# RWKV and SGU trunk on one Trainium2 core: three more slots in the shared pool, an output projection unit split earlier, and four bank lists

## The chip, the cores and the metric

The kernel runs on one core of a Trainium2 chip. The time is device time in microseconds (us) from launch to the last instruction; the median of several runs counts. The kernel before takes 1320.23 us (three runs, 1316.43 to 1321.08).

The engines are named as in the profile: PE multiplies matrices into the eight banks of PSUM, DVE and ACT work element by element and move sums out of PSUM, POOL masks and fills, and SP issues nearly all DMAs. Every engine takes its instructions strictly in the order that was fixed when the program was built.

## The reference

Two layers on 512 tokens of width 1024, each a mixer and a SwiGLU feed-forward net, every sub-layer between two RMS norms. Layer 0 mixes with an RWKV-7 scan over 16 heads of 64, layer 1 with a gated product over blocks of 128 tokens. What matters here is the end of layer 0's mixer:

```python
def step(S, inp):
    r_t, w_t, k_t, v_t, a_t, b_t = inp
    sa = jnp.einsum('bhij,bhj->bhi', S, a_t)
    S = (S * w_t[:, :, None, :]
         + sa[..., None] * b_t[:, :, None, :]
         + v_t[..., None] * k_t[:, :, None, :])
    y = jnp.einsum('bhij,bhj->bhi', S, r_t)
    return S, y
...
y = _rwkv7_scan(r_h, decay, k_h, v_h, -kk, kk * a_h)
y = (y - mu) * lax.rsqrt(var + GN_EPS)                  # per head
y = y * gn_w + gn_b
y = y + jnp.sum(r_h * k_h * r_k, axis=-1, keepdims=True) * v_h
return (y * g) @ w_o
...
x = x + _rmsnorm(h, norm_gains[i, 1])
h = _rmsnorm(x, norm_gains[i, 2])
h = (jax.nn.silu(h @ w_gate) * (h @ w_up)) @ w_down
```

## The kernel before

All products keep nearly full float32 accuracy by three passes: each operand is split into a rounded part and the rest (`split`, L181 on ACT, L182 on DVE), and `mm3` (L206) adds three of the four products. So every weight tile is loaded (`wraw`), cast by ACT (`whi`) and subtracted by DVE (`wlo`) before PE can use it. `weight()` does this for one unit: a load of 512 KB, then the two halves of the split. `wraw`, and each pair of `whi` and `wlo`, have two buffers.

The scan is worked out in chunks of 64 tokens, for batches of 4 heads (b = 0 to 3; "B1" is the back of batch 1). The stages of a batch are:

- P and E: projections, decays and scaled operands, written to DRAM (`sa`, `sb`).
- F, `front`: loads four `MV` tiles (L988) and builds four `BX` tiles, one for each of 4 units, all 4 KB a partition from the shared pool `s` (`slot`, L175 to 178, with `SLOTS` tiles); then the key products `lm` (L1004) in the banks `pl`, from which ACT copies into `MV`, `LA` and `BX`, POOL masks, and PE transposes `bkt` (L1018).
- B, `back`: the inverse of each chunk's triangular matrix. DVE turns `LA` into `LX` (L1035), runs a loop of 30 small operations on `Dm` (L1049, L1051), and turns the result twice, into `hn` (L1054) and `Dt` (L1055). Then follows a chain of small products on PE with a copy by DVE or ACT behind each: Qp (L1071), `Qs` (L1074), Np (L1080) and Tp (L1083), their copies `Dn` (L1086) and `bdT` (L1088), Q2p (L1094), its copies (L1097, L1098), T2p (L1103), and the merge `bdT<-T2p` (L1107). Behind it, unit by unit, `mp` (L1112), its copy `MVt`, `gh` (L1119) and the adds into `MV` (L1121, L1122). `MVt` is first filled by the transposes `mvt` (L1062, bank list `pl`).
- S, the scan over 8 chunks: `us` (L1148), `su` (L1150, L1153), `Yp` (L1161).
- N, `finish`: group norm (L1177 to L1185), bonus, the transposes `vt` (L1198) and `yt` (L1223), gate (L206, L1227), and for b = 0 to 2 a store to `od`, which the projection loads again (`oraw`, L1281) and splits into `oT`.
- V, the value projection, gives PE work beside B0. Its `xs` (the shifted input) holds 4 slots of the pool until V3 is done.

`PLAN` (L35) gives the order in which these are written in the program. The sequence on each engine is not that order: the framework's scheduler fixes it at build time from its own estimates of durations, buffers and banks, so that a change of a pool's size or of a bank can move instructions over a wide stretch.

The output projection is `out_proj` (L287). It sums 8 k tiles for 4 token tiles into the banks of `h0` (columns 0 to 511) and later `h1` (columns 512 to 1023). `unit(half, u)` loads and splits the weights of two k tiles, and with `after` the scheduler is told to issue these no sooner than B3's merges (`merged0`, `merged1`, L1107). `acts(k)` gives `oT`. At its end each token tile is normed and transposed (`ptr`, L281, banks `tr`, copied out by L62 on ACT and L64 on DVE) for the feed-forward net, whose gate and up products `gu` begin in the banks of `gu`.

What is fixed by hand and touched by the change: `SLOTS`, `PLAN`, and the bank lists `BANKS_RWKV` and `BANKS_F0` (L28 to L30), in which the `pl` banks are 1 and 2, `pt` (the small products of the inverse) 3 and 4, `pb` 5 and 6, and `us`, `yp`, `mp` the banks 0, 7 and 5.

## Time and profile before

| what | value |
|---|---|
| median of 3 runs | 1320.23 us (1316.43 to 1321.08) |
| profiled execution | 1315.28 us |
| its span, first to last instruction | 1313.6 us |
| mean granted clock of PE | 0.984 |
| PE / weight loads / DVE / ACT / POOL busy | 96% / 83% / 75% / 56% / 12% |
| DMA, mean over the span | 110 GB/s, 144.29 MB |

A row of the timeline gives the start and the length in us, the engine, the line of the kernel, the operation, output<-input by tile names, the shape and the count; in brackets stand the idle time before it and what ended that. A row of the waits gives the engine and line that waited, what it waited for, the sum in us, the number of waits and the longest. PE's clock is granted in steps: at half rate a matrix product takes about twice as long, and the mean over a stretch is given as a share of full speed.

The page's slices show where PE is not at full use; each digit is one fortieth of the span (32.8 us) in tenths:

```profile
PE   5999999989899899999999999999989999999998
PEclk9999999999979999999999999999989999999999
```

The RWKV stages end near 380 us (twelfth slice), the output projection runs to 455 us (fourteenth), and then come the first feed-forward net, the gating unit and the second net.

### The profile page before, as it was taken

How to read it: one execution, taken by the hardware profiler on the slowest of the kernel's cores; microseconds unless marked ns; L12 is line 12 of the kernel's file. 1: busy time of each engine (PE TensorE's matmuls, PEld its weight loads, DVE VectorE, ACT ScalarE, POOL GpSimd, SP SyncE). 2: the span in 40 equal slices, each digit the busy share in tenths (PEclk: the TensorE clock that was granted, in tenths of full speed). 3: DMA queues.
4: the chain of work that ended last, by engine and by line, in shares of the span. 5: the costliest groups of instructions: out<-in, count | busy, mean ns of one | idle time of the engine just before them, and what ended most of it. 6: DMA issues, size and time to landing. Idle time of an engine off the chain costs nothing.

```text
span 1313.6 us, 24404 instructions
## 1 busy us (share of the span) xinstructions
PE 1257.4 (96%) x9644; PEld 1091.1 (83%) x9644; DVE 988.1 (75%) x1613; ACT 739.4 (56%) x1303; POOL 151.6 (12%) x300
## 2 busy tenths in 40 slices
PE   5999999989899899999999999999989999999998
...
PEclk9999999999979999999999999999989999999999
...
GB/s 163 34 95 175 146 224 156 88 72 65 75 127 112 75 80 160 68 126 125 92 154 136 122 49 128 94 135 94 144 97 1 129 98 105 120 125 149 113 65 81
DMA packets 219379, 144.29 MB, mean 110 GB/s; under 512 B 67920, under 2 KB 193408, under 8 KB 219264
## 3 DMA queue, kind: packets, MB, share of 16 engines
...
q8 instruction: 76, 1.25, 0.4%
...
## 4 chain that ended last, share of the span: by engine, by line
PE 68%; DVE 7%; ACT 2%; issue 1%; DMA 1%; POOL 0%; DVEq 0%; ACTq 0%
PE acc L206 25%; PE Q L206 10%; PE gu L206 9%; PE R L206 7%; PE Z L206 7%; PE u L206 3%; DVE wlo L182 1%; PE gh L1119 1%; PE mp L1112 1%; PE Yp L1161 1%; PE lm L1004 1%; DVE wsum L405 1%; DVE x L336 1%; PE s L1366 1%; PE ptr L281 0%
## 5 line engine op out<-in xcount | busy, mean ns | idle before, releaser
L182 DVE TENSOR_TENSOR wlo<-wraw,whi 128x1024 fp32r<-128x1024 f32 x83 | 103.1, 1244 | 66.5 <-ACT whi L181 57.7
L206 PE MATMUL Q<-bc,whi 128*128 128x256 f32 x816 | 147.3, 281 | 2.2 <-ACT hn L449 2.2
L206 PE MATMUL acc<-whi,ablk 128*128 128x512 f32 x448 | 141.6, 395 | 2.7 <-DVE acc L623 2.7
L181 ACT CAST whi<-wraw 128x1024 fp32r<-128x1024 f32 x83 | 86.9, 1050 | 101.5 <-PE acc L206 29.2
L206 PEld LDWEIGHTS Q<-bc,whi 128*128 128x128 f32 x816 | 125.5, 189 | 2.8 <-ACT hn L449 2.6
L181 ACT CAST whi<-wsum 128x1024 fp32r<-128x1024 f32 x68 | 71.1, 1051 | 85.0 <-PE Q L206 24.3
L206 PE MATMUL gu<-hT,whi 128*128 128x256 f32 (+1 forms) x448 | 112.0, 342 | 3.3 <-ACT hT L62 1.7
L206 PE MATMUL Q<-bc,wlo 128*128 128x256 f32 x408 | 114.6, 281 | 0.0
L206 PEld LDWEIGHTS acc<-whi,ablk 128*128 128x128 f32 x448 | 84.2, 188 | 23.3 <-ACT hn L621 1.8
L206 PE MATMUL Z<-bc,whi 128*128 128x256 f32 x544 | 99.8, 281 | 0.0
L206 PE MATMUL R<-bc,whi 128*128 128x256 f32 x544 | 98.7, 281 | 0.0
L182 DVE TENSOR_TENSOR wlo<-wsum,whi 128x1024 fp32r<-128x1024 f32 x68 | 82.2, 1221 | 21.5 <-ACT whi L181 20.4
L181 ACT CAST whi<-wq 128x1024 fp32r<-128x1024 f32 x51 | 53.5, 1050 | 72.3 <-PE R L206 22.9
L206 PEld LDWEIGHTS gu<-hT,whi 128*128 128x128 f32 x448 | 78.8, 197 | 13.7 <-ACT hT L62 2.4
L206 PE MATMUL acc<-wlo,ablk 128*128 128x512 f32 x224 | 88.5, 395 | 1.5 <-DVE wlo L182 1.5
L182 DVE TENSOR_TENSOR wlo<-wq,whi 128x1024 fp32r<-128x1024 f32 x51 | 65.3, 1284 | 27.6 <-ACT whi L181 27.4
L206 PEld LDWEIGHTS Z<-bc,whi 128*128 128x128 f32 x544 | 84.1, 189 | 0.0
L206 PEld LDWEIGHTS R<-bc,whi 128*128 128x128 f32 x544 | 83.8, 188 | 0.2
L206 PE MATMUL proj<-xsp,whi 128*128 128x512 f32 x256 | 82.4, 401 | 1.3 <-ACT r L813 1.3
L206 PEld LDWEIGHTS Q<-bc,wlo 128*128 128x128 f32 x408 | 77.2, 189 | 0.0
L206 PE MATMUL Z<-bc,wlo 128*128 128x256 f32 x272 | 76.3, 282 | 0.9 <-DVE wlo L182 0.9
L206 PE MATMUL R<-bc,wlo 128*128 128x256 f32 x272 | 76.6, 282 | 0.0
...
## 6 DMA issues: line engine op xcount, KB each, us to landing
...
```

The lines of the kernel that those rows point to most:

```text
L181: self.nc.scalar.copy(hi, src)
L182: self.nc.vector.tensor_tensor(lo, src, hi.bitcast(F32), op=ALU.subtract)
L206: self.nc.tensor.matmul(out, l, r, start=start, stop=stop, skip_group_check=resumed)
L336: v.scalar_tensor_tensor(xts[tt][:, c], f, y[:, 0:1], xts[tt][:, c], op0=ALU.mult, op1=ALU.add)
L405: v.tensor_tensor(s, x, y, op=ALU.add)
L1004: mm(lm[:, cc * P:(cc + 1) * P], st[:, cc].rearrange("p n t -> p (n t)"), mv[:, cc, :, hd, :], start=True, stop=True)
L1112: mm(mp[:, cc * P:(cc + 1) * P], bdT[:, q * NC + 4 * hh + cc].rearrange("p h t -> p (h t)"), mt[:, cc, :], start=True, stop=True)
L1119: mm(gh[:, cc * P:(cc + 1) * P], mt[rows, cc, :], bx[rows, 0:2, cc, :], start=True, stop=True)
L1161: mm(yp[yr, yc], MV[hh, q][:, cc, 1, hd, :], su[:, q, hd, :], start=True, stop=True)
L1366: mm(acc[:, tt * P:(tt + 1) * P], vt[tt][:, m * P:(m + 1) * P], wsT[:, m, :], start=True, stop=True)
```

## The change

- `SLOTS` goes from 17 to 20. Two fronts hold 8 tiles each (4 `MV`, 4 `BX`), and `xs` 4. The room, 12 KB a partition, comes from `dynamic_dma_scratch_size=4096`, the space for the descriptors of DMAs that POOL issues (9 in this kernel: the gains, and vectors and weights of the gating unit).
- `PLAN` gets "W1" behind "S0": the first unit of the output projection's weights (k tiles 0 and 1, columns 0 to 511) is loaded and split there, in the `wp` buffers that V has left, and is handed to `out_proj` as `ready`. The other units are issued behind B3's merges as before.
- `h0` becomes (1, 2, 5, 7): the first two token tiles' sums go into the banks of the key products (`pl`), which nobody needs behind F3 and its `mvt`. Before, the second tile's sum had bank 3, of B3's small products. `h1` and the banks of `gu` in the first feed-forward net are permuted to fit.

```diff
--- before.py
+++ after.py
@@ -26,13 +26,13 @@
 LN_EPS = 1e-5
 LN_HALF = -0.6931471805599453
 BANKS_RWKV = dict(pa=(0,), pl=(1, 2), pt=(3, 4), pb=(5, 6), pe=(0, 7, 3, 4), us=(0,), yp=(7,), mp=(5,), pf=(6,),
-                  h0=(1, 3, 5, 7), h1=(2, 4, 0, 6), tr=(1, 2))
-BANKS_F0 = dict(tr=(1, 2), gu=(3, 4, 7, 6), R=(3, 4), Q=(5, 0), Z=(7, 6), h0=(1, 2, 4, 0), h1=(3, 5, 7, 6))
+                  h0=(1, 2, 5, 7), h1=(4, 6, 0, 3), tr=(1, 2))
+BANKS_F0 = dict(tr=(1, 2), gu=(4, 6, 3, 7), R=(3, 4), Q=(5, 0), Z=(7, 6), h0=(1, 2, 4, 0), h1=(3, 5, 7, 6))
 BANKS_SGU = dict(tr=(1, 2), pa=(3, 5, 7, 6), h0=(1, 2, 4, 0), h1=(3, 5, 7, 6))
 BANKS_F1 = dict(tr=(1, 2), gu=(4, 0, 7, 6), R=(4, 0), Q=(3, 5), Z=(7, 6), h0=(1, 2, 0, 5), h1=(4, 3, 7, 6))
-SLOTS = 17
+SLOTS = 20
 E2 = 7
-PLAN = "P0 E0 P1 E1 P2 E2 P3 E3 X0 F0 B0 F1 V0 V1 V2 V3 B1 S0 F2 S1 F3 N0 B2 N1 B3 S2 N2 S3 N3".split()
+PLAN = "P0 E0 P1 E1 P2 E2 P3 E3 X0 F0 B0 F1 V0 V1 V2 V3 B1 S0 W1 F2 S1 F3 N0 B2 N1 B3 S2 N2 S3 N3".split()
 XV = "xxxessss"
 XSLOTS = 13
 LAG = 2
@@ -284,7 +284,7 @@
     def prenorm(self, col):
         return Norm(self, col)
 
-    def out_proj(self, acts, wrows, nk, row, xts, store=None, tail=3, norm=None, spare=None, mid=None, after=(), begun=None):
+    def out_proj(self, acts, wrows, nk, row, xts, store=None, tail=3, norm=None, spare=None, mid=None, after=(), begun=None, ready=()):
 
 
         nc = self.nc
@@ -303,6 +303,9 @@
 
         def unit(half, u):
             own = spare if half and u < nu - late[1] else None
+            if not half and u < len(ready):
+                hi, lo = ready[u]
+                return [(2 * u + j, (hi[:, j, :], lo[:, j, :])) for j in range(2)]
             with ExitStack() as order:
                 for ins in after:
                     order.enter_context(self.tc.issue_after(ins.ins))
@@ -1246,6 +1249,7 @@
             g_hidden()
             xk = mixed_split(1, "xxxxssss")
             xr, kr, ops, Y = None, {}, {}, {}
+            wo, begun_w = i["rwkv_w_o"][0].rearrange("(u j p) n -> u p j n", p=P, j=2), []
             for n in PLAN:
                 f, b = n[0], int(n[1])
                 if f == "P":
@@ -1262,6 +1266,8 @@
                     front(b, ops[b])
                 elif f == "B":
                     back(b, ops[b])
+                elif f == "W":
+                    begun_w.extend(self.weight(wo[u][:, :, 0:512]) for u in range(b))
                 elif f == "S":
                     if b == 3:
                         GW.append(gate_weights(b))
@@ -1289,9 +1295,8 @@
             xts = [self.xp.tile([P, D], F32, name="x", tag="x", bufs=TT) for _ in range(TT)]
             for t in range(TT):
                 nc.sync.dma_start(out=xts[t], in_=i["x"][0, t * P:(t + 1) * P, :])
-            wo = i["rwkv_w_o"][0].rearrange("(u j p) n -> u p j n", p=P, j=2)
             norm = self.prenorm("g02")
-            self.out_proj(acts, lambda u: wo[u], KT, i["norm_gains"][0, 1], xts, norm=norm, spare=e2, after=(ops[3]["merged0"], ops[3]["merged1"]))
+            self.out_proj(acts, lambda u: wo[u], KT, i["norm_gains"][0, 1], xts, norm=norm, spare=e2, after=(ops[3]["merged0"], ops[3]["merged1"]), ready=begun_w)
             return xts, norm
 
 
@@ -1417,7 +1422,7 @@
     import concourse.bacc as bacc
     from concourse.bass_utils import run_bass_kernel_spmd
 
-    nc = bacc.Bacc("TRN2", target_bir_lowering=False, num_devices=1)
+    nc = bacc.Bacc("TRN2", target_bir_lowering=False, num_devices=1, dynamic_dma_scratch_size=4096)
     arrays, ins = {}, {}
     for name in _INS:
         arr = np.ascontiguousarray(inputs[name])
```

The number of instructions on each engine is the same. PE's order is the same up to about 207 us, and behind about 470 us only neighbours change places. Between these, the following has moved.

DVE in B1's chain, from `Qs` on. Before:

```order
L1074 TENSOR_TENSOR Qs<-Qp,id_144 128x512
L1150 TENSOR_TENSOR su<-us,pc 64x2x64
L1088 COPY bdT<-Tp 32x16x32 x2
L1098 COPY Q_2991<-Q2p 32x512
L1177 TENSOR_REDUCE mu<-Y 128x16
L1178 TENSOR_SCALAR mu<-mu 128x16
L1179 TENSOR_TENSOR Y<-Y,mu 128x1024
L1183 TENSOR_REDUCE va<-hn 128x16
L1107 COPY bdT<-T2p 32x16x32
```

After (lines are 3 higher):

```order
L1077 TENSOR_TENSOR Qs<-Qp,id_144 128x512
L1153 TENSOR_TENSOR su<-us,pc 64x2x64
L1091 COPY bdT<-Tp 32x16x32 x2
L1153 TENSOR_TENSOR su<-us,pc 64x2x64
L1101 COPY Q_2991<-Q2p 32x512
L1153 TENSOR_TENSOR su<-us,pc 64x2x64
L1110 COPY bdT<-T2p 32x16x32
L1153 TENSOR_TENSOR su<-us,pc 64x2x64
L1124 TENSOR_TENSOR MV<-gh,BX 128x4x64
L1125 TENSOR_TENSOR MV<-gh,MV 128x4x64
L1180 TENSOR_REDUCE mu<-Y 128x16
```

The group norm's rows (`mu`, `Y`, `va`) stood between the copy `Q` and the merge `bdT<-T2p`; now the merge stands ahead of them. At the other end of B1, LX stood behind three pairs of the adds `MV` of B0, and stands right behind B0's merge now. Behind B1, LX of B2 now comes after the group norm of batch 0 has begun and after the adds of B1; LX of B3, all of its loop and two `oT` splits stand among the copies of B2's chain, ahead of its merge.

PE in B2's chain, from Q2p on to the first `mp`. Before:

```order
L1018 MATMUL bkt<-ident,ST 128x128 x4
L1094 MATMUL Q2p<-Dn_4024,LA 32x32
L1062 MATMUL mvt<-ident,MV 128x128 x4
L1094 MATMUL Q2p<-Dn_4024,LA 32x32 x18
L1062 MATMUL mvt<-ident,MV 128x128 x8
L1103 MATMUL T2p<-bdT,Q_4064 32x32 x19
L1062 MATMUL mvt<-ident,MV 128x128 x4
L1103 MATMUL T2p<-bdT,Q_4064 32x32 x13
L1198 MATMUL vt<-ident,hn 128x128 x4
L1062 MATMUL mvt<-ident,MV 128x128 x8
L1198 MATMUL vt<-ident,hn 128x128 x4
L1112 MATMUL mp<-MVt,bdT 128x128 x4
```

After:

```order
L1086 MATMUL Tp<-Dt,Qs 32x32 x64
L1097 MATMUL Q2p<-Dn_4030,LA 32x32 x32
L1201 MATMUL vt<-ident,hn 128x128 x4
L1106 MATMUL T2p<-bdT,Q_4070 32x32 x32
L1201 MATMUL vt<-ident,hn 128x128 x4
L1115 MATMUL mp<-MVt,bdT 128x128 x4
L1226 MATMUL yt<-ident,Y 128x128 x4
```

The transposes `bkt` and `mvt` that lay between the small products are now ahead of Tp (most of them inside Qp), with all of F3's key products. Before these rows, Np and Tp were mixed with key products and scan steps; now Tp is one piece.

PE in B3's chain, from the scan steps behind Qp on. Before:

```order
L1148 MATMUL us<-su,MV 64x64 x4
L1161 MATMUL Yp<-su,MV 64x64 x4
L1080 MATMUL Np<-Qs,Dt 32x32 x32
L1083 MATMUL Tp<-Dt,Qs 32x32 x64
L1094 MATMUL Q2p<-Dn_4507,LA 32x32 x32
L1148 MATMUL us<-su,MV 64x64 x4
L1161 MATMUL Yp<-su,MV 64x64 x5
```

After, with the program's numbers of the tiles, since the sums would read alike without them (`acc_5109` and `acc_5110` are the first two token tiles, `whi_3234` and `wlo_3235` the unit that was split early; two rows ahead and two behind are left out, the last sums go on with `oT_5130`):

```order
L1164 MATMUL Yp_4720<-su_4709,MV_3240 64x64 x2
L1164 MATMUL Yp_4720<-su_4709,MV_3245 64x64 x2
L206 MATMUL acc_5109<-whi_3234,oT_5115 128x512
L206 MATMUL acc_5109<-wlo_3235,oT_5115 128x512
L206 MATMUL acc_5109<-whi_3234,oT_5115 128x512
L206 MATMUL acc_5110<-whi_3234,oT_5115 128x512
L206 MATMUL acc_5110<-wlo_3235,oT_5115 128x512
L206 MATMUL acc_5110<-whi_3234,oT_5115 128x512
L206 MATMUL acc_5109<-whi_3234,oT_5130 128x512
L206 MATMUL acc_5109<-wlo_3235,oT_5130 128x512
L206 MATMUL acc_5109<-whi_3234,oT_5130 128x512
L206 MATMUL acc_5110<-whi_3234,oT_5130 128x512
```

Twelve sums stand between the scan steps behind Qp and Np; before, the first sum came behind T2p, one ahead of `mp` and eleven behind it.

At the end of the projection, before, PE's rows were: 27 sums, 3 transposes `ptr` of tile 0, 2 sums, 5 `ptr`, 7 sums, 8 `ptr` of tile 1, and then `gu`. After, they are: 8 `ptr` of tile 0, 36 sums, 8 `ptr` of tile 1, 26 products `gu`, 4 `ptr` of tile 2, `gu`.

## Prediction, made before the changed kernel was run

> **What bounds the kernel now.** I read the page first, then the waits of PE, then the granted clock by stretches, then PE's and DVE's timelines around the places found.
>
> ```profile
> PE 1257.4 (96%) x9644; PEld 1091.1 (83%) x9644; DVE 988.1 (75%) x1613; ACT 739.4 (56%) x1303; POOL 151.6 (12%) x300
> PE ptr L281 <- DVE hn L736: 7.5, 1, 7.5
> PE ptr L281 <- ACT hn L737: 5.6, 1, 5.6
> ```
>
> PE is busy for 96% of the span of 1313.6 us. The change adds and removes no PE work, so it can gain only where PE stands still or runs at a lower clock. 1313.6 − 1257.4 = 56 us are idle, of which 7.5 + 5.6 = 13 are the two first waits of the program, which the change does not reach. The rest is small waits, and behind them stretches at half clock:
>
> ```profile
> 225.00:240.00 15.00, 13.31 (x380) 12.82 (x379) 2.75 (x4) 7.28 (x16) 3.52 (x9) 0.89 0.06 20
> 285.00:300.00 15.00, 14.44 (x116) 13.13 (x117) 13.90 (x34) 9.04 (x19) 11.55 (x26) 0.89 0.09 20
> 315.00:330.00 15.00, 14.25 (x366) 12.10 (x355) 7.67 (x14) 12.54 (x34) 10.68 (x28) 1.00 0.28 81
> 330.00:345.00 15.00, 12.15 (x139) 10.27 (x138) 14.47 (x43) 7.19 (x13) 1.17 (x2) 0.89 0.09 32
> 360.00:375.00 15.00, 13.00 (x375) 12.02 (x376) 6.56 (x13) 9.35 (x20) 0.41 (x2) 0.53 0.15 33
> 450.00:465.00 15.00, 11.19 (x63) 9.40 (x62) 13.33 (x39) 10.90 (x30) 0.00 (x0) 0.89 0.36 105
> ```
>
> The columns are the stretch, its length, busy us of PE, weight loads, DVE, ACT and POOL, then the granted clock, the DMA share and GB/s. The rows from 225, 285, 330 and 360 hold the chains of the triangular inverses of batches 0 to 3 (B0 to B3), the last one the end of the output projection. A clock of 0.89 over 15 us is 0.11 × 15 × 2 = 3.3 us at half rate, which costs half of that, 1.7; 0.53 in B3 is 14 us, which cost 7. These places, 225 to 465 us, are what the change can move; from 470 us on the new order differs from the old by swaps of neighbours alone.
>
> **The change part by part.** Three more slots let a front (loads, key products) start before an older one's buffers come free, and the scheduler reorders B1, B2 and B3 with it.
>
> *B1.* These are rows of DVE, then of PE:
>
> ```profile
> 243.47 0.42 DVE L1121 TENSOR_TENSOR MV<-gh,BX 128x256 f32<-128x256 f32 x1 [5.99 <-PE gh L1119]
> 249.75 0.42 DVE L1121 TENSOR_TENSOR MV<-gh,BX 128x256 f32<-128x256 f32 x1 [4.85 <-PE gh L1119]
> 250.42 1.98 DVE L1035 STREAM_TRANSPOSE LX<-LA 128x1024 f32<-128x1024 f32 x1
> 279.36 1.22 DVE L1177 TENSOR_REDUCE mu<-Y 128x16 f32<-128x1024 f32 x1
> 283.56 1.22 DVE L1183 TENSOR_REDUCE va<-hn 128x16 f32<-128x1024 f32 x1 [1.18 <-ACT hn L1181]
> 284.81 0.69 DVE L1107 COPY bdT<-T2p 32x512 f32<-32x512 f32 x1
> 268.69 1.28 PE L1071 MATMUL Qp<-hn,LA 32*32 32x32 f32 x128 [0.47 <-DVE hn L1054]
> 270.56 0.30 PE L1161 MATMUL Yp<-su,MV 128*64 128x64 f32 x2 [0.60 <-issue]
> 275.95 0.59 PE L1083 MATMUL Tp<-Dt,Qs 32*32 32x32 f32 x46 [0.78 <-issue]
> 280.10 1.20 PE L1103 MATMUL T2p<-bdT,Q 32*32 32x32 f32 x64
> 285.56 1.77 PE L1112 MATMUL mp<-MVt,bdT 128*128 128x128 f32 x8 [2.24 <-DVE bdT L1107]
> ```
>
> Before, LX of B1 stands on DVE behind three pairs of adds that wait for PE, and DVE idles 5.99 + 4.85 us there. Now LX comes right behind B0's merge, since F1's key products are done by then, and B1's inverse can start earlier by up to 10.8 us of idle time; PE lets about half of it be used, since 8 of F2's key products and the scan of batch 0 still stand ahead of Qp. At the other end the group norm of batch 0 sat on DVE ahead of the merge `bdT<-T2p`: T2p ended at 281.3, the copy began at 284.81, PE waited 2.24, and 3.3 us at half clock followed. In the new order the group norm is behind the merge. The waits removed sum to 2.24 + 0.78 + 0.60 + 0.47 and 1.7 for the clock, 5.8. I take **−6**, ends 0 (DVE late for another reason) and −8 (with some of the other idle time).
>
> *B2.* The group norm and the adds that left B1's chain now stand before and in B2's:
>
> ```profile
> 324.12 1.95 DVE L1035 STREAM_TRANSPOSE LX<-LA 128x1024 f32<-128x1024 f32 x1 [0.53 <-POOL LA L972]
> 327.09 0.66 PE L1018 MATMUL bkt<-ident,ST 128*128 128x128 f32 x4
> 332.00 0.76 PE L1103 MATMUL T2p<-bdT,Q 32*32 32x32 f32 x36 [0.84 <-DVE Q L1098]
> 337.38 0.69 DVE L1107 COPY bdT<-T2p 32x512 f32<-32x512 f32 x1
> 338.12 1.16 PE L1112 MATMUL mp<-MVt,bdT 128*128 128x128 f32 x8 [0.52 <-DVE bdT L1107]
> 347.20 2.12 DVE L1054 STREAM_TRANSPOSE hn<-Dm 128x1024 f32<-128x1024 f32 x1
> ```
>
> From B1's merge (284.81) to B2's (337.38) pass 52.6 us. The work that the new order has on DVE between the two merges is 51.5 us, with the durations that the same rows have before. So B2's merge can follow B1's in the same time only if DVE is idle for 1.1 us in all; today it idles 7.3 of 15 us from 315 to 330 alone, where it waits for PE's scan steps. LX of B3 (1.95), its loop of 30 small operations, and two `oT` splits, which wait for a store and a load of `od`, now stand among the chain's copies. And PE has less to put between: before, 4 bkt and 24 mvt passes stood between Tp and `mp`, 28/4 × 0.66 = 4.6 us; now they are done ahead of Tp, and 8 vt passes, 1.3 us, are left. I take **+4**, that is two thirds of B1's gain given back. The ends are −2 (DVE keeps the lead, and the waits of 0.84 and 0.52 go) and +10 (4.6 for the cover, two more stretches at half clock at 1.7, and 2.12 if `hn` of B3 lands in the chain).
>
> *B3.* This is where the early weight unit and the two banks act:
>
> ```profile
> 360.10 1.25 PE L1080 MATMUL Np<-Qs,Dt 32*32 32x32 f32 x61 [1.44 <-DVE Qs L1074]
> 361.79 1.14 ACT L181 CAST oT<-oraw 128x512 fp32r<-128x512 f32 x2 [2.80 <-DMA oraw<-od]
> 364.48 0.42 PE L1083 MATMUL Tp<-Dt,Qs 32*32 32x32 f32 x12 [1.47 <-issue]
> 365.08 1.92 PE L1094 MATMUL Q2p<-Dn,LA 32*32 32x32 f32 x64 [0.18 <-ACT Dn L1086]
> 369.94 1.91 PE L1103 MATMUL T2p<-bdT,Q 32*32 32x32 f32 x62
> 443.22 0.39 PE L206 MATMUL acc<-wlo,oT 128*128 128x512 f32 x1
> 443.45 0.39 PE L206 MATMUL acc<-whi,oT 128*128 128x512 f32 x1
> ```
>
> Twelve sums of the output projection now stand between Qp and Np. From start to start one takes 443.45 − 443.22 = 0.23 us, so they are 2.8 us of work. They fill the wait of 1.44 and push Np back by the other 1.4, to 361.5. That push is free: Q2p waits for `Dn`, which ACT copies only behind the `oT` casts, and these waited 2.80 us for a DMA until 361.79; the new order leaves that queue as it was. So Q2p stays near 365, with 2.8 us of later work already done. What else there is to gain is the clock: T2p takes 1.91 here against 1.20 in B1. Of the 7 us that half clock costs I let one stretch of 3.3 go, 1.7 at most, and count somewhat under that: **−4**. The ends are −1 (the twelve sums take the place of idle time that comes back later) and −8 (the clock stays full up to `mp`).
>
> [...]
>
> *The end of the projection.* Before, PE ran out of sums while the normed activations were transposed:
>
> ```profile
> 454.89 0.66 PE L281 MATMUL ptr<-ident,x 128*128 128x128 f32 x4 [0.55 <-DVE hT L64]
> 456.64 0.66 PE L281 MATMUL ptr<-ident,x 128*128 128x128 f32 x4 [1.09 <-DVE hT L64]
> 458.24 0.62 PE L206 MATMUL gu<-hT,whi 128*128 128x256 f32 x3 [0.95 <-ACT hT L62]
> 460.07 0.58 PE L206 MATMUL gu<-hT,whi 128*128 128x256 f32 x1 [1.21 <-DVE hT L64]
> ```
>
> Tile 0's eight transposes now stand 36 sums (36 × 0.23 = 8.3 us) ahead of tile 1's, and the gate and up products start in banks that the first tiles' sums have left. The first two waits are covered, 1.64; of the other two, 2.16, and of the 1.7 of half clock that they bring, I count somewhat over a third, 1.4: **−3**, ends 0 and −5.
>
> *At nothing:* the early load and split. The split's 1.2 us on DVE and its cast on ACT fall into or ahead of B0's stretch, where DVE is busy for 2.75 of 15 us; without that cover they would cost 1.2. One more weight load stands in SP's queue ahead of the front's loads; these waited for slots there and no longer do, so the queue has the time. The smaller descriptor space serves DMAs that POOL issues, of which no one is on the chain: 0 (ends 0 and +2). The gate and up banks belong to the item above.
>
> Sum: −6 + 4 − 4 − 3 = **−9 us**. The profiled execution took 1315.28, so one like it would take 1306; the runs shown have the median 1320.23 (1316.43 to 1321.08), so I take the same step from there: **1311 us**.
>
> **The rivals.** *B2 takes it all.* If DVE idles between the merges as it does now, B2 costs +8; with B3's clock as low as before (−1) the sum is −6 + 8 − 1 − 3 = −2: **1318**. For it speaks that 1.1 us is all the slack; against it, that the wait at B2's `mp` is only 0.52 today.
>
> *DVE keeps its lead.* B1's whole gain goes on to B3 (−8 − 2 − 6 − 3 = −19): **1301**. For it speaks that DVE's idle time of 5.99 and 4.85 us is real; against it, that the 51.5 us must then run without a gap.
>
> *Slower: the bare chain in B2.* Between Tp and `mp` PE has only 1.3 us of other work left. If DVE is late there by a block of 2 us (an `hn`, an LX) at each of three copies, as the group norm made it in B1, PE stands 6 us, the 4.6 us taken out as cover have been spent where nothing was idle, and four stretches run at half clock (4 × 1.7 = 6.8): +17 in B2, with −6, −1 and −1 elsewhere +9: **1329**. It decides from a price of B2 of 14 on. Against it: B3, as bare today, loses 7 to the clock and 3.1 to waits, 10.
>
> *It doesn't do what it says.* If the twelve sums wait for their banks or for `oT`, Np stands behind them, since PE takes its instructions in order, and the inverse is late: +2 in B3 and a sum of −3, **1317**. The splits of batch 0's `oT` stand in B2's chain, well before, so this is unlikely, and I count it with the first rival.
>
> **How the numbers follow.** The forecast has 0.50 (its own range 1305 to 1316), B2 takes it all or B3 fails 0.28, DVE keeps its lead 0.12, slower 0.10. 0.5% is 6.6 us, about what a measurement of this kernel can tell from no change. Faster by more, below 1313.6: 0.46 of the first case and all of the third, 0.58. Within: 0.04, the 0.28 and 0.02 of the last, 0.34. Slower: 0.08. The range of 8 in 10 leaves out the slower case and the better part of the third: **1301 to 1321**.
>
> **What would show it.** B1: `mp`'s first wait for `bdT` under 0.5 us, at 276 to 278, and no half clock behind it. B2: the merge less than 5 us earlier than 337.38, and waits of PE from Tp to `mp` of over 3 us. B3: twelve sums between Qp and Np without a wait, Q2p still released by ACT's `Dn`, the clock of its 15 us above 0.6. End: the waits at the transposes gone and `gu` entered with at most one wait. The forecast is wrong if B2's merge is more than 5 us earlier (then lower), or if PE loses in B2 more than B1 gained (then higher).

## The result, and the profile after

The changed kernel takes **1330.62 us** (median of four runs, 1328.99 to 1332.54) against 1318.33 us (four runs, 1314.71 to 1321.08) for the kernel before: ratio **1.0103, 95% interval 1.0083 to 1.0122**. It is slower by 1%, where 0.7% faster was forecast. The profiled execution took 1329.26 us with a span of 1327.6 us, 14.0 us more than before. Of the profiles below one, that of e7, was taken in a slow execution (1350.26 us; its other three runs took 1330.21 to 1335.04), so only its order and its waits are read.

The page's line of busy times and the granted clock by stretches of the changed kernel, in the columns that the prediction explains; the stretches are those around the same chains, which now come up to 11 us later:

```profile
PE 1262.7 (95%) x9644; PEld 1096.3 (83%) x9644; DVE 988.3 (74%) x1613; ACT 738.2 (56%) x1303; POOL 151.9 (11%) x300
...
225.00:240.00 15.00, 12.24 (x348) 11.72 (x336) 3.66 (x5) 7.80 (x18) 5.96 (x15) 0.77 0.21 57
255.00:270.00 15.00, 12.94 (x240) 11.44 (x241) 10.20 (x25) 5.87 (x17) 6.10 (x15) 0.89 0.28 85
270.00:285.00 15.00, 12.38 (x376) 11.16 (x374) 2.40 (x5) 9.43 (x25) 5.26 (x14) 0.77 0.22 49
330.00:345.00 15.00, 8.49 (x330) 7.19 (x328) 12.99 (x34) 7.17 (x15) 0.36 (x2) 0.74 0.35 100
345.00:360.00 15.00, 13.65 (x113) 11.42 (x109) 12.70 (x27) 4.45 (x9) 0.00 (x0) 0.80 0.05 19
375.00:390.00 15.00, 13.52 (x224) 11.93 (x225) 6.26 (x10) 7.56 (x16) 0.41 (x2) 0.66 0.20 55
465.00:480.00 15.00, 13.54 (x89) 12.86 (x88) 14.46 (x52) 11.54 (x39) 0.00 (x0) 0.77 0.36 106
1035.00:1050.00 15.00, 11.96 (x79) 11.89 (x79) 12.11 (x12) 5.06 (x6) 0.00 (x0) 0.77 0.40 110
```

B0 and B1 (the rows from 225 and 270) went from 0.89 to 0.77: 0.23 x 15 x 2 = 6.9 us at half clock each, two stretches where there was one, and one more stands ahead of B1 (255), where the clock was full before. B2 (330 to 360) has 0.26 and 0.20, 13.8 us, against 3.3 before. Only B3 (375) is better, 0.66 for 0.53. The last row is new: the second feed-forward net lost clock, where before nothing happened.

PE's waits from 220 to 390 us, the changed kernel (what waited, for what, sum, number, longest):

```profile
PE Tp L1086 <- issue: 6.7, 4, 2.8
PE vt L1201 <- DVE hn L1198: 4.4, 1, 4.4
PE Yp L1164 <- DVE su L1153: 2.1, 1, 2.1
PE Q2p L1097 <- issue: 1.9, 1, 1.9
PE mp L1115 <- DVE bdT L1110: 1.3, 1, 1.3
```

8.6 us of these stand at "issue", where PE waited for nothing that the profile shows; in the same chains of the kernel before it is 5.3. The rest of these rows is DVE.

Where the 14 us lie, by PE's lost time: the length of a stretch less what its products need at their dense pace (the median from start to start of the same product in the trace of before). It holds waits and half clock together.

| stretch (B0's Qp to its mp, and so on) | lost before | after | difference | the prediction's term |
|---|---|---|---|---|
| start to B0's Qp | 31.2 | 30.2 | -1.0 | 0 |
| B0, Qp to mp | 5.4 | 7.0 | +1.6 | 0 |
| to B1's Qp | 3.4 | 5.8 | +2.4 | -6, with the next row |
| B1, Qp to mp | 6.9 | 8.9 | +2.0 | |
| to B2's Qp | 3.4 | 4.3 | +0.9 | +4, with the two next rows |
| B2, Qp to mp | 10.9 | 14.6 | +3.7 | |
| to B3's Qp | 1.4 | 2.5 | +1.1 | |
| B3, Qp to mp | 9.6 | 6.4 | -3.2 | -4 |
| to 15 us behind the first gu | 15.4 | 17.0 | +1.6 | -3 |
| to the second net's gu | 12.5 | 12.3 | -0.2 | 0 |
| second net, first 90 us | 2.9 | 7.1 | +4.2 | 0 |
| to the end | 3.0 | 3.9 | +0.9 | 0 |

From B0's first Qp to B3's first `mp` the differences sum to +8.5. PE's waits of over 0.15 us grew there from 13.1 to 18.3 us, of which those at issue by 3.3. The other 3.3 us are work that ran slower than its dense pace: the time at half clock in that stretch grew from 23.4 to 37.2 us. The table compares one profile with one; how far profiles of one order differ is said where it matters.

Rows of the changed kernel's timelines that carry most of it, six of PE and three of DVE:

```profile
233.13 0.44 PE L1086 MATMUL Tp<-Dt,Qs 32*32 32x32 f32 x16 [2.76 <-issue]
264.12 0.33 PE L1164 MATMUL Yp<-su,MV 128*64 128x64 f32 x2 [2.05 <-DVE su L1153]
277.16 1.17 PE L1097 MATMUL Q2p<-Dn,LA 32*32 32x32 f32 x36 [1.90 <-issue]
287.89 0.60 PE L1115 MATMUL mp<-MVt,bdT 128*128 128x128 f32 x3
464.78 1.32 PE L281 MATMUL ptr<-ident,x 128*128 128x128 f32 x8 [2.52 <-DVE x L339]
1038.11 0.58 PE L206 MATMUL Z<-bc,whi 128*128 128x256 f32 x1 [3.04 <-DVE bc L182]
...
260.11 2.05 DVE L1057 STREAM_TRANSPOSE hn<-Dm 128x1024 f32<-128x1024 f32 x1
262.06 1.89 DVE L1058 STREAM_TRANSPOSE Dt<-Dm 128x1024 f32<-128x1024 f32 x1
263.79 0.28 DVE L1153 TENSOR_TENSOR su<-us,pc 64x128 f32<-64x128 f32 x1
```

`mp` of B1 at 287.89 has no wait any more: the merge's 2.24 us went, as predicted. But B1's chain did not get shorter. From its first Tp to `mp` pass 15.7 us, against 11.3 before. And at 264.12 stands the price of the earlier inverse: the scan's `su` is queued on DVE behind `hn` and `Dt` of B1, which came forward past it, so that PE waits 2.05 us.

At 464.78 PE waits once for the normed tile, 2.52, where the prediction saw the first two of four small waits covered; of the other two, at `gu`, 0.37 and 1.09 us are left. At 1038.11 it waits 3.04 us in the second net for the split of `bc`. Two rows of DVE there show why:

```profile
1034.56 1.23 DVE L408 TENSOR_TENSOR wsum<-wq 128x1024 f32<-128x1024 f32 x1 [2.77 <-DMA wq<-in_ffn_w_up_dram]
...
1036.84 1.22 DVE L182 TENSOR_TENSOR bc<-tsum,bc 128x1024 fp32r<-128x1024 f32 x1
```

DVE stands 2.77 us before a sum of weights whose load has not come, and the split of `bc`, which PE waits for, is behind it. In the kernel before, the split stood ahead of that sum. This is one of the "swaps of neighbours" behind 470 us.

### The profile page after: what moved, and what is told of

Its sections match the earlier page's. It is cut to its first block, busy times and chain, and to the rows that moved or that the text cites. A ratio compares the mean times of both kernels' runs of the same rounds, so it can differ in the third digit from the quotient of the medians.

```text
span 1327.6 us, 24401 instructions
## 1 busy us (share of the span) xinstructions
PE 1262.7 (95%) x9644; PEld 1096.3 (83%) x9644; DVE 988.3 (74%) x1613; ACT 738.2 (56%) x1303; POOL 151.9 (11%) x300
## 3 DMA queue, kind: packets, MB, share of 16 engines
q8 instruction: 76, 1.25, 0.4%
## 4 chain that ended last, share of the span: by engine, by line
PE 74%; DVE 13%; ACT 4%; issue 4%; DMA 4%; SPq 1%; POOL 0%; DVEq 0%; ACTq 0%
PE acc L206 23%; PE Q L206 10%; PE Z L206 7%; PE gu L206 7%; PE R L206 6%; PE proj L206 5%; PE u L206 3%; DVE wlo L182 3%; PE v L206 2%; PE lm L1007 2%; PE gh L1122 1%; PE Yp L1164 1%; DVE wsum L408 1%; ACT whi L181 1%; DVE xs L769 1%
## 5 line engine op out<-in xcount | busy, mean ns | idle before, releaser
L206 PE MATMUL Z<-bc,whi 128*128 128x256 f32 x544 | 102.5, 286 | 3.0 <-DVE bc L182 3.0
L182 DVE TENSOR_TENSOR wlo<-wsum,whi 128x1024 fp32r<-128x1024 f32 x68 | 82.3, 1222 | 19.4 <-ACT whi L181 18.3
L206 PEld LDWEIGHTS gu<-hT,whi 128*128 128x128 f32 x448 | 77.4, 193 | 13.1 <-DVE hT L64 2.9
```

Of the source, the lines that this page charges most:

```text
L182: self.nc.vector.tensor_tensor(lo, src, hi.bitcast(F32), op=ALU.subtract)
L206: self.nc.tensor.matmul(out, l, r, start=start, stop=stop, skip_group_check=resumed)
```

## The experiments

Eighteen kernels. Each was timed beside the kernel before on the same chip; the ratio is to that. A diff shows what is edited, against the changed kernel or, where said, the kernel before.

### Which part of the change loses the time

**e1**: 20 slots and the smaller descriptor space, on the kernel before; no early unit, old banks.

```diff
-SLOTS = 17
+SLOTS = 20
-    nc = bacc.Bacc("TRN2", target_bir_lowering=False, num_devices=1)
+    nc = bacc.Bacc("TRN2", target_bir_lowering=False, num_devices=1, dynamic_dma_scratch_size=4096)
```

> Before, with twenty slots and the smaller descriptor space, but without the early weight unit and with the old banks. The order of the instructions in the chains of B0, B1 and B2 is that of the changed kernel; B3's chain and the second feed-forward net have the order of before. Theory (the slots' new order is what costs): PE loses in the trace of the changed kernel 11.7 us more than before from Qp of B0 to Qp of B3, so this kernel should be slower than before by 10 to 12 us, ratio 1.0075 to 1.009. Rival (the slots cost nothing, and the early unit, the banks or the late net cost): within 2 us of before, ratio 0.9985 to 1.0015.

Measured: 1330.84 us, ratio 1.0096 [1.0067, 1.0125], the whole loss of the change. It has the changed kernel's losses around B1 and in B2: 5.8 to B1's Qp, 8.5 in B1, 15.4 in B2. B0, in the changed kernel's order, loses 5.3 and has one stretch at half clock, as before. B3 loses 9.3 (9.6 before), and the first 90 us of the second net lose no more than before.

**e2**: the changed kernel with 17 slots, so the early unit and the four bank lists alone.

```diff
-SLOTS = 20
+SLOTS = 17
```

> The changed kernel with 17 slots: early weight unit, new banks, smaller descriptor space. The chains of B0 to B2 and the second feed-forward net have the order of before; twelve sums stand between Qp and Np of B3. Theory: only B3's gain is left, 3.2 us by the changed kernel's trace, and up to 2 more or less at the end of the projection: 2 to 5 us faster than before, ratio 0.996 to 0.9985. Rival (early unit or banks cost, as one more load and split stand ahead of B0's chain): slower than before by 2 us or more, ratio over 1.0015.

Measured: 1319.06 us, ratio 1.0012 [0.9985, 1.0039], no difference. B0 to B2 are as before within 0.5. B3 loses 5.5 for 9.6, a gain of 4.1, just the -4 of the prediction. But from B3's `mp` to the gate products 15.5 are lost for 12.3, and in the 15 us behind, 4.9 for 3.0: the gain is given back. Waits of PE in e2 from 374.7 to 464.7 us, behind B3's `mp`:

```profile
PE ptr L281 <- DVE hT L64: 2.5, 1, 2.5
PE Yp L1164 <- ACT Y L1166: 2.0, 1, 2.0
PE gu L206 <- DVE hT L64: 1.9, 1, 1.9
```

The last scan steps wait 2.0 us for ACT, and from 414.7 to 424.7 the clock is 0.83, 3.4 us at half. PE has one wait of 2.5 and one of 1.9 at the end of the projection in place of four of 0.55 to 1.21.

**e10**: the early unit alone, with 17 slots and the old banks and descriptor space (the diff is against the kernel before; the code that hands the unit over and the edit of e3, below, are in it too).

```diff
-PLAN = "... V3 B1 S0 F2 ...".split()
+PLAN = "... V3 B1 S0 W1 F2 ...".split()
```

> 17 slots, the old banks and the old descriptor space; the early weight unit alone, with the order of e3 in the second FFN. Six sums of the projection (1.4 us) stand between Qp and Np of B3. Theory (the sums drawn forward lie in time that B3 loses; what e2 gave back at the projection's start came of the sums of two tiles missing there, which the new banks let go forward): B3 loses 7 to 8.5 against 9.6 before, the stretch from mp to gu 12 to 13.5 against 12.3; ratio 0.997 to 1.000. Rival (each sum drawn forward is missing behind mp, wherever its bank is): the stretch from mp to gu loses what B3 gains, 1.4 to 3 more, ratio 0.9995 to 1.002.

Measured: 1319.51 us, ratio 1.0012 [0.9995, 1.0029]. B3 lost 8.5 (9.6 before), and the stretch behind it 15.0 (12.3 before). That is the rival's number; but e11, which draws no sum forward, lost 15.0 there as well, so a single profile does not show that the missing sums are the cause.

**e4**: the smaller descriptor space alone, on the kernel before; its order is that of before.

```diff
-    nc = bacc.Bacc("TRN2", target_bir_lowering=False, num_devices=1)
+    nc = bacc.Bacc("TRN2", target_bir_lowering=False, num_devices=1, dynamic_dma_scratch_size=4096)
```

> Before, with nothing but the smaller descriptor space for the DMAs that POOL issues; every engine has the order of before. Theory (the descriptor space is of no account): the same time as before, ratio 0.9985 to 1.0015. Rival (POOL's DMAs or the fetches of instructions suffer from it): slower by 3 us or more, ratio over 1.002.

Measured: 1315.48 us, ratio 0.9991 [0.9962, 1.0021]. It costs nothing that shows; e1's loss is the slots'. Its profile also shows how far one order can spread: B0 lost 1.3 us more than in the kernel before, with 6.8 us at half clock for 3.4.

### The second feed-forward net

**e3**: the changed kernel, with the weight sum of that one place queued on DVE behind the split of `bc`.

```diff
...
-            o["s"] = wsum(o["a21"], o["a22"])
+            with ExitStack() as order:
+                if li == 1 and n == first + 1:
+                    order.enter_context(self.tc.issue_after(quads.done[5].ins))
+                o["s"] = wsum(o["a21"], o["a22"])
...
```

(`quads.done[5]` is that split; the lines that record it are left out.)

> The changed kernel with one constraint more for the scheduler: in the second feed-forward net the weight sum that waits for a load is issued behind the split of bc, as before. Elsewhere no instruction changes its place. Theory (in the changed kernel DVE waits there 2.8 us for the load, PE waits 3.0 for bc, and half clock follows): faster than the changed kernel by 4 to 6 us, so slower than before by 6 to 9, ratio 1.0045 to 1.007. Rival (the late load is chance, or the time comes back later): as the changed kernel, ratio 1.009 to 1.011.

Measured: 1330.09 us, ratio 1.0084 [1.0048, 1.0121]. The 6.0 us lost from 50 to 90 us of that net are 0.3, so the cause of the wait is shown (0.1 to 1.0 in the later kernels with this edit, but 3.7 in e5, where `Z` waits for another split); over its first 90 us 3.9 are lost for 7.1 (2.9 before). The total does not show it: the ten runs spread from 1319 to 1337, and in the profiled one the stretch from B0's `mp` to B1's Qp lost 9.7 for 5.8, with the same order. Seven kernels with one order up to there (e3, e6, e9, e12, e14, e15, e18) lost 5.1 to 9.7 in it. So a difference of 2 us in one stretch of one profile proves little, and the readings below need either a place or several runs.

All further kernels with 20 slots contain this edit.

### The waits at "issue"

In six traces (before, after, e1 to e4) the longer waits inside the chains fell on the same numbers of the matmul in PE's program, counted from the start, within 6, whatever stood there. After has them at 1485, 2242, 3111 and 3745. The trace's DMA part has two queues that bring instructions, q14 with 39 transfers, 0.32 MB, and this one:

```profile
q8 instruction: 76, 1.25, 0.4%
```

On q8, 76 transfers, 1.25 MB, so 16 KB each; PE has 9644 matmuls and as many weight loads, and 2 x 9644 / 76 = 254, so I take q8 for PE's. Each of these waits ends 1.2 to 1.6 us after a transfer of q8 has landed. A wait at issue need not be of this kind: that of `Yp` in B1 (0.56 to 0.60 us in before, e2 and e4) ends about 8 us after the last landing.

**e5**: shift the program by half a piece.

```diff
         nc.gpsimd.memset(self.ones, 1.0)
+        dummy = self.ps.tile([P, 512], F32, name="dummy", tag="b6", bufs=1)
+        for _ in range(32):
+            nc.tensor.matmul(dummy[0:32, 0:32], self.ident[0:32, 0:32], self.ident[0:32, 0:32], start=True, stop=True)
```

> The kernel of e3 with 32 small products (32x32, 64 passes with 64 weight loads) at PE's very start, while it waits for its first data; every engine's order is otherwise that of e3. The products' result is used by nothing. Theory (the stalls in the chains are PE waiting for its own instructions, which come in pieces of 256): each such stall moves back by exactly 64 passes in the program. In e3 they stand in B0 behind 102 passes of Tp, in B1 behind 28 of Q2p, in B2 behind 123 of Tp, in B3 behind 105 of Tp; here they should stand behind 38 of Tp, 92 of Tp, 59 of Tp and 41 of Tp (each within 3), with lengths of 1 to 3 us, and nothing at the old places but what a next piece brings. Rival (a stall belongs to the work at its place: the half clock, a bank, a weight): the stalls stay where they are in e3, within 3 passes. The time may go either way by up to 6 us, since only the places move: 1322 to 1336.

PE's timeline of e3, then of e5, the rows in the chains that waited for issue (the count behind x is what ran from the wait on; Tp has 128 passes, Q2p 64):

```profile
232.19 0.44 PE L1089 MATMUL Tp<-Dt,Qs 32*32 32x32 f32 x16 [1.80 <-issue]
280.50 1.17 PE L1100 MATMUL Q2p<-Dn,LA 32*32 32x32 f32 x36 [1.06 <-issue]
340.38 0.25 PE L1089 MATMUL Tp<-Dt,Qs 32*32 32x32 f32 x3 [2.35 <-issue]
378.91 0.53 PE L1089 MATMUL Tp<-Dt,Qs 32*32 32x32 f32 x21 [1.61 <-issue]
```

```profile
233.03 0.95 PE L1092 MATMUL Tp<-Dt,Qs 32*32 32x32 f32 x88 [0.53 <-issue]
236.60 0.57 PE L1103 MATMUL Q2p<-Dn,LA 32*32 32x32 f32 x25 [1.97 <-issue]
276.17 0.50 PE L1092 MATMUL Tp<-Dt,Qs 32*32 32x32 f32 x35 [2.30 <-issue]
334.27 0.77 PE L1092 MATMUL Tp<-Dt,Qs 32*32 32x32 f32 x67 [1.50 <-issue]
338.11 0.32 PE L1103 MATMUL Q2p<-Dn,LA 32*32 32x32 f32 x3 [2.08 <-issue]
378.88 0.53 PE L1103 MATMUL Q2p<-Dn,LA 32*32 32x32 f32 x22 [1.06 <-issue]
```

The waits stand behind 38 passes of Tp in B0, 91 in B1 and 59 in B2; predicted were 38, 92 and 59 (two passes of Tp that run among those of Np are left out of the counts). In B3 nothing is at 41 of Tp, and the next piece, 127 passes on, waits at 42 of Q2p. So the place is set by the number of the instruction, not by the work there. The time, 1329.53 us, ratio 1.0107 [1.0078, 1.0136], is no better: B1 lost 6.4 instead of 8.8, B3 9.5 instead of 7.2.

**e11**: the same 32 products in the kernel before.

> The kernel of before with the 32 small products of e5 at PE's start; every other order is that of before. Theory (pieces of 256 instructions): the stalls inside the chains move back by 64 passes: B0 from behind 13 passes of Q2p to behind 77 of Tp, B1 from 80 of Tp to 16 of Tp, B2's out of Q2p into Tp or its fillers, B3 from 114 of Tp to 50 of Tp, each within 3 and 0.7 to 2.5 us long. The time: between 1312 and 1322, since some boundaries come to lie in waits and others out of them. Rival: they stay where they are in before.

Measured: 1321.83 us, ratio 1.0028 [0.9996, 1.0060]. The waits moved to 75 of Tp in B0 (77 predicted) and 50 of Tp in B3 (50); in B1 only 0.25 us stands at 16 of Tp (16 predicted), and the next piece, 128 on, waits 1.68 us at 18 of Q2p. B2's wait in Q2p is gone, and a gap at two passes of T2p stayed where it was, so that one is of another kind. B1 lost 10.4 instead of 6.9; with 1.09 us at Qp it has three such waits, 3.0 us, where the kernel before has 1.0.

### B2

In all kernels below, merge to merge is DVE's second copy `bdT<-T2p` of B1 to that of B2, "other work" is PE's from the first Tp to `mp` that is not the chain's own 2.6 us, "DVE's other" the durations of what DVE does from Tp to its merge beside the chain's 2.8 us, summed (neighbouring rows overlap, so the sum is above the busy time).

| | merge to merge | Tp to mp | other work | DVE's other | lost, Qp to mp | ratio |
|---|---|---|---|---|---|---|
| before | 52.6 | 15.8 | 5.4 | 13.1 | 10.9 | 1 |
| after | 61.7 | 14.7 | 1.0 | 12.5 | 14.6 | 1.0103 |
| e3 (order as after) | 60.8 | 13.7 | 1.0 | 12.5 | 13.7 | 1.0084 |
| e6 filler out | 59.8 | 13.0 | 0 | 11.3 | 13.9 | 1.0099 |
| e9 cover in, with a bank's wait | 63.1 | 16.6 | 2.9 | 13.2 | 16.2 | 1.0129 |
| e12 cover in | 61.9 | 16.9 | 2.9 | 13.2 | 16.0 | 1.0091 |
| e14 cover in, filler out | 61.6 | 15.2 | 1.9 | 11.1 | 15.6 | 1.0123 |
| e15 DVE's loop out | 58.8 | 11.7 | 1.0 | 8.7 | 11.7 | 1.0090 |
| e18 loop out, cover in | 58.6 | 14.6 | 2.9 | 8.7 | 11.6 | 1.0124 |

**e6**: the largest single wait of B2, 4.38 us of `vt`, stands in PE's queue ahead of T2p and waits for DVE. The products with `hn` that feed it are queued behind B2's merge.

```diff
                 obs = []
+                order = ExitStack()
+                for n in (0, 1) if b == 1 else ():
+                    order.enter_context(self.tc.issue_after(ops[2]["merged%d" % n].ins))
                 for q in range(2):
                     v.tensor_tensor(Vn[:, :, q], ...)
...
+                order.close()
                 return obs
```

> The kernel of e3 with the bonus of batch 1 (its load, the two products on DVE and the eight vt passes on PE) issued only behind B2's two merges, so that none of it stands between Q2p and mp of B2. Theory (a filler that itself waits for DVE stands in PE's queue ahead of T2p and holds it): vt's wait (4.38 us in the changed kernel's profile, 2.7 in e3's) is gone, T2p waits for Q alone; lost in B2 from Qp to mp 9 to 11 us against 13.7 and 14.6; time 1322 to 1328, ratio 1.004 to 1.009. Rival (B2 lost its cover, and that is the cost): with 1.3 us less of other work between Tp and mp, B2 loses as much as before or more, 13.5 to 16, and the ratio stays at 1.009 or over.

Measured: 1329.84 us, ratio 1.0099 [1.0069, 1.0129]. PE's two longest waits of e6 from B2's first Tp to `mp`:

```profile
PE T2p L1109 <- ACT bdT L1094: 3.8, 1, 3.8
PE mp L1118 <- DVE bdT L1113: 2.2, 1, 2.2
```

and the last two copies of `bdT` ahead of T2p, of DVE and of ACT:

```profile
346.38 0.69 DVE L1094 COPY bdT<-Tp 32x512 f32<-32x512 f32 x1
347.10 0.58 ACT L1094 COPY bdT<-Tp 32x512 f32<-32x512 f32 x1 [2.04 <-DVE bdT L1094]
```

The filler's wait is gone, and T2p itself waits 3.8 us in the same place, for copies of `bdT` that DVE and ACT make in turn and of which DVE's came late. The rival was right: 13.9 lost. The wait with the largest number was not the cause; it stood where T2p would have waited.

**e7**: e6, and the group norm of batch 1 behind the merge too.

```diff
-                group_norm(Y, tts)
+                with ExitStack() as order:
+                    for n in (0, 1) if b == 1 else ():
+                        order.enter_context(self.tc.issue_after(ops[2]["merged%d" % n].ins))
+                    group_norm(Y, tts)
```

> As e6, with the group norm of batch 1 too issued behind B2's merges; DVE then has only the triangular loop of B3 (small operations under 0.5 us) and two oT splits among B2's copies. Theory (what is left of B2's loss is DVE's copies standing behind long operations): the merge's wait at mp goes (1.3 us), B2 loses 7 to 9; but the norm's 10 us now stand in or ahead of B3, whose Dt follows it, so that B3's Qp is reached up to 3 us later or B3 loses up to 3 more; time 0 to 4 us under e6. Rival (no cover): as for e6, B2 at 13.5 or more. Rival (DVE is the bound there, not the order): the sum of what is lost from B1's mp to B3's mp is the same as in e6 within 1 us, the loss only moves.

Measured: 1334.85 us, ratio 1.0126 [1.0093, 1.0160]. T2p still waits 3.0 us for `bdT` and `mp` 2.5 for the merge. In the place of the norm, B3's loop and `Dt` came forward on DVE.

**e9** and **e12**: put cover back. Half of B2's `mvt` passes are written behind Q2p and queued behind the last Tp (e9). In e12, B3's `mvt` passes are held behind B2's last T2p as well.

```diff
...
+                for hh in range(2 - late, 2):
+                    with self.tc.issue_after(last.ins):
+                        turn(hh)
                 T2p = self.bank("pt", "T2p")
...
```

(`turn(hh)` is the old `mvt` loop for one half, `late` is 1 for B2, `last` the last Tp.)

> The kernel of e3 with half of B2's mvt passes (those of the second half of the chunks) issued only behind its last Tp, so that 16 mvt passes (4 x 0.58 = 2.3 us of PE work, 8 of them B2's) stand between Q2p and T2p again. Theory (B2 lost its cover: from Tp to mp the chain of copies takes 13 to 15 us whatever PE does in it, and the slots took 4.4 of the 5.4 us of other work out): from Tp to mp 13.5 to 15 us as in e3, the other work in it 1.0 -> 3.3 us, lost from Qp to mp 10.5 to 12 against 13.7; time 1324 to 1329, ratio 1.006 to 1.010. Rival (PE's queue or DVE's lengthens with what is put in, as B1's did, 11.3 -> 15.7 us with 2.2 us more): from Tp to mp 16 us or more and 13.5 or more lost, ratio as e3's or over.

Measured, e9: 1335.63 us, ratio 1.0129 [1.0095, 1.0163]. Its third `mvt` unit waited 3.7 us for its bank, since the key products have only two; so e9 tells nothing of cover.

> e9 with B3's mvt passes held behind B2's last T2p: only the 8 mvt passes of B2's second half (1.2 us) stand between Q2p and T2p, in the two banks that are free there, so that none waits for a bank. Theory (cover): the wait of 3.7 us of e9 goes; from Tp to mp 13.5 to 15 us, the other work in it 2.2 us (1.0 in e3) before the 8 of B3 behind T2p are counted, lost in B2 11.5 to 13 against 13.7 in e3 and 16.2 in e9; ratio 1.007 to 1.011. Rival (what is put in comes on top of the chain): 15 us or more from Tp to mp, 14 or more lost.

Measured, e12: 1326.65 us, ratio 1.0091 [1.0068, 1.0114]. The bank's wait is gone, but the stretch is longer by more than what was put in, and 16.0 are lost. The rival was right again. The next rows give, for the kernel before, the changed one and e12, the stretch from B2's first Tp to `mp`:

```profile
322.30:338.10 15.80, 12.86 (x329) 10.78 (x322) 14.01 (x30) 11.52 (x25) 6.90 (x15) 0.89 0.27 82
```

```profile
333.10:347.80 14.70, 7.06 (x281) 5.91 (x274) 13.56 (x34) 7.25 (x13) 0.00 (x0) 0.64 0.24 68
```

```profile
333.80:350.70 16.90, 12.04 (x286) 10.85 (x287) 15.19 (x39) 9.08 (x16) 0.00 (x0) 0.50 0.24 77
```

In all three DVE is busy for nearly the whole stretch (14.01 of 15.80, 13.56 of 14.70, 15.19 of 16.90). Before, PE had 12.86 us of work beside it; after, 7.06. In e12 it has 12.04, but at half clock throughout (0.50), where the same passes take 1.6 to 1.9 times as long: in the trace of the changed kernel the 64 passes of T2p take 1.20 us at full clock and 1.92 at half, four transposes 0.66 and 1.12, and `mp` starts every 112 ns and every 213.

**e14**: e12 and e6 together.

> e12 with the bonus of batch 1 behind B2's merge too (as e6): the mvt passes are B2's only other work from Tp to T2p, and none of them waits for DVE. Theory (cover must be work that is ready): from Tp to mp 12.5 to 14 us, lost in B2 10.5 to 12. Rival (the chain's length is DVE's queue, which holds the group norm and two oT splits, whatever PE does): from Tp to mp 13.5 to 15.5, lost 12 to 14, within 1 us of e6's 13.9.

Measured: 1331.59 us, ratio 1.0123 [1.0089, 1.0156]; 15.6 lost, T2p waits 5.1 us for `bdT`. The theory of the cover falls with it. What is left is DVE, and its rows in the changed kernel behind B1's merge show what happened there:

```profile
285.37 0.69 DVE L1110 COPY bdT<-T2p 32x512 f32<-32x512 f32 x1
287.90 0.28 DVE L1153 TENSOR_TENSOR su<-us,pc 64x128 f32<-64x128 f32 x1 [1.84 <-PE us L1151]
292.44 0.42 DVE L1124 TENSOR_TENSOR MV<-gh,BX 128x256 f32<-128x256 f32 x1 [4.27 <-PE gh L1122]
...
293.12 1.21 DVE L1180 TENSOR_REDUCE mu<-Y 128x16 f32<-128x1024 f32 x1
...
301.60 1.98 DVE L1038 STREAM_TRANSPOSE LX<-LA 128x1024 f32<-128x1024 f32 x1
```

and in the kernel before:

```profile
285.53 1.72 DVE L1195 TENSOR_TENSOR hn<-hn,bn 128x512 f32<-128x512 f32 x2
...
288.63 1.38 DVE L1185 TENSOR_TENSOR Y<-Y,nr_y 128x1024 f32<-128x1024 f32 x1
290.32 1.98 DVE L1035 STREAM_TRANSPOSE LX<-LA 128x1024 f32<-128x1024 f32 x1 [0.31 <-POOL LA L972]
```

Before, DVE did the group norm of batch 0 and LX of B2 right behind B1's merge, beside PE's `mp`. After, it stands idle there, 1.84 + 4.27 us, because the norm is queued behind the adds `MV<-gh`, which wait for PE; LX comes 11 us later. From there on DVE catches up until B2's merge.

**e15**: take work off DVE: B3's LX and with it its loop are queued behind B2's merge; PE's order stays.

```diff
-                v.transpose(full(LX), LA.rearrange("p q c (x t) -> p t (q c x)", x=2))
+                with ExitStack() as order:
+                    if b == 3:
+                        order.enter_context(self.tc.issue_after(ops[2]["merged1"].ins))
+                    v.transpose(full(LX), LA.rearrange("p q c (x t) -> p t (q c x)", x=2))
```

> The kernel of e3 with B3's LX and its loop of 30 small operations queued on DVE behind B2's second merge; PE's order in B2 stays that of e3 up to T2p (the eight vt passes fall behind T2p). Theory (DVE sets B2's end: between the merges of B1 and B2 it is busy for 51 us, with 9.5 to 10.5 us of idle time ahead of that which nothing filled): about 9 us of DVE's work leave this stretch (1.95 for LX and some 13 pairs of 0.55), so merge to merge 60.8 -> 51 to 54 us, from Tp to mp 13.7 -> 9 to 11.5, lost in B2 6 to 10 against 13.7; B3 gets the same work in a row (some 14 us with its two transposes), so its Qp is reached with 0 to 6 us more lost. Ratio 0.999 to 1.008. Rival (B2's length is its chain of copies, the missing cover and the stalls, not DVE's load): merge to merge 59 or more, from Tp to mp 12.5 or more.

Measured: 1326.17 us, ratio 1.0090 [1.0060, 1.0120]. From merge to merge, the changed kernel and e15:

```profile
285.40:347.00 61.60, 54.59 (x864) 46.62 (x862) 49.96 (x120) 44.42 (x111) 32.33 (x78) 0.92 0.22 60
```

```profile
286.00:344.70 58.70, 53.86 (x863) 46.32 (x862) 43.03 (x94) 43.88 (x110) 29.18 (x70) 0.94 0.23 63
```

DVE is busy 6.9 us less, and the stretch is 2.9 us shorter (2.0 against e3's 60.8); B2 loses 11.7, 2.0 less than e3 and near before's 10.9. Profiles of the changed kernel's order in B2 (after, e1, e3, e5) lost 13.7 to 15.4, and e18, with the same DVE order as e15, 11.6, so part of B2's loss is DVE's load. It is not all of the stretch: 4.0 of the 6.9 us that DVE was spared came back as idle time, as PE's dense work holds the chain's start (Tp at 47.8 us behind B1's merge, as in after). B3's Qp then came with 5.7 lost instead of 2.7, and in the total no gain shows: 1.0090 against e3's 1.0084.

**e18**: e15 and e12 together.

> e15 and e12 together: B3's LX and loop behind B2's merge on DVE, and the 8 mvt passes of B2's second half between Q2p and T2p on PE, B3's 8 behind T2p. Theory (two limits for B2 from Tp to mp, the longer one counts: DVE's load, which e15 cut from 15.2 to 11.5 us, and the chain of copies, some 11 to 12 us; cover helps only where the chain is the longer one, so not in e12): from Tp to mp 11 to 13 us, the merge 0.5 to 2 us nearer to B1's than in e15 (58.8), lost in B2 8.5 to 10.5 against 11.7 in e15 and 16.0 in e12. Rival (work put behind Tp always comes on top): from Tp to mp 13.5 or more, lost 11.5 or more, merge to merge as in e15 or longer. The time: ratio 1.005 to 1.010 by either, as B3 pays for the loop.

Measured: 1331.81 us, ratio 1.0124 [1.0107, 1.0140]; 11.6 lost, as in e15, and 14.6 us from Tp to `mp`. T2p's wait is 0.5 us now, but Q2p waits 2.6 for instructions, and the clock is 0.65. The cover gains nothing beside it: my theory of two limits is not borne out.

### The first chains

**e8**: the last two of F1's four units are held where 17 slots had them: their copies on ACT are queued behind B0's merge.

```diff
+                order = ExitStack()
                 for hh, q in units:
+                    if b == 1 and (hh, q) == units[2]:
+                        for n in (0, 1):
+                            order.enter_context(self.tc.issue_after(ops[0]["merged%d" % n].ins))
...
+                order.close()
```

> The kernel of e3 with the last two of F1's four units of key products issued behind B0's merges, about where 17 slots had them; the slots stay 20. B0's chain then has v products again where it had lm and bkt in Q2p to T2p; B1's chain gets the group norm of batch 0 back. Theory (what stands at a boundary of 256 instructions decides): B0's stall behind 102 passes of Tp stays at 2 to 3 us, as nothing ahead of it changes, so B0 still loses 6.5 to 7; B1's stall goes back to 80 passes into Tp with 0.8 to 1.2 us, and the merge's wait of 2 us comes back: B1 loses 7 to 8 against 8.8; mp of B0 to Qp of B1 loses 3 to 5 against 5.8 and 9.7. Time 1322 to 1329. Rival (the key products drawn forward took B0's cover, and that alone is what B0 lost): B0 loses 5.4 again, as before, without a stall in Tp.

Measured: 1327.56 us, ratio 1.0087 [1.0058, 1.0116]. From B0's `mp` to B1's Qp 3.5 are lost, as before (3.4), and the wait of `Yp` for `su` is gone; e13, which has the same edit, lost 3.5 as well, while the eleven other kernels with 20 slots and early units (after, e1, e3, e5, e6, e9, e12, e14 to e16, e18) lost 5.1 to 9.7. So that wait comes from B1's inverse being drawn forward past the scan. B0 lost 5.8 with the wait at 102 passes of Tp still there (1.5 us): between theory and rival. B1 lost 9.7, with 2.0 at issue and the merge's wait back. B2, of which the expectation says nothing, lost 11.7 for e3's 13.7, and its merge came 53.7 us behind B1's (52.6 before): with the group norm of batch 0 ahead of B1's merge again, B2 has nearly its old length. But to B3's Qp 4.9 are lost (2.5 after) and in B3 9.9 (6.4 after), more than B2 gains.

**e13**: e8 and e12 together.

> e12 and e8 together: B2's cover back, and F1's last two units' copies behind B0's merges; the slots stay 20. Theory (the slots' loss is cover and DVE order, place by place): B0 5.5 to 6, from its mp to B1's Qp 3.5, B1 7 to 10 (its stall by chance), B2 10 to 12, B3 6.5 to 10; sum from B0's Qp to B3's Qp 31 to 36 against 43 in the changed kernel and 31.4 before; time 1320 to 1327, ratio 1.003 to 1.008. Rival (the losses only move along the chain, since one DVE does all of it): the sum stays at 39 or more, ratio 1.008 or over.

Measured: 1330.61 us, ratio 1.0116 [1.0091, 1.0141]. From B0's Qp to B3's Qp 43.5 are lost, against 43.1 after, 39.9 in e8 and 31.4 before. The rival was right: repairs at single places do not add up.

### DVE's work on another engine

**e16**: the group norm's two products with Y for batches 0 and 1 on POOL; **e17**: the same in the kernel before.

```diff
-            def group_norm(Y, tts):
+            def group_norm(Y, tts, e=v):
...
-                v.tensor_tensor(y4, y4, mu.unsqueeze(2)...
+                e.tensor_tensor(y4, y4, mu.unsqueeze(2)...
...
-                v.tensor_tensor(y4, y4, rs.unsqueeze(2)...
+                e.tensor_tensor(y4, y4, rs.unsqueeze(2)...
...
-                group_norm(Y, tts)
+                group_norm(Y, tts, g if b in (0, 1) else v)
```

> The kernel of e3 with the two products of the group norm with Y (Y less its mean, Y by its scale) of batches 0 and 1 on POOL instead of DVE. Theory (DVE's load): four operations of 1.22 us leave DVE between the merges of B1 and B2, merge to merge 60.8 -> 55 to 59 us, lost in B2 10 to 13; on POOL one takes between 1.2 and 5 us (no row shows it), and the selections of F3 wait behind it. Ratio 1.003 to 1.009. Rival (the gaps only move, or POOL is the later one): merge to merge 60 or more, ratio 1.008 or over.

> The kernel of before with the same four products on POOL. Theory: in B1 the group norm of batch 0 then no longer holds the merge (wait of 2.24 us at mp), and B2, where DVE has 15.8 us of work in the 15.1 us from Tp to its merge, gets 2.4 us less: merge to merge of B1 and B2 52.6 -> 49 to 52; time 1308 to 1316, ratio 0.994 to 1.000. Rival (POOL's time is on the path, or PE has nothing to do with the time won): ratio 1.002 or over.

Measured: e16 1345.92 us, ratio 1.0220 [1.0192, 1.0249]; e17 1321.83 us, ratio 1.0054 [1.0034, 1.0074]. POOL's groups from 240 to 400 us in e16 (busy, mean ns of one, idle before):

```profile
L1185 POOL TENSOR_TENSOR Y<-Y,mu 128x1024 f32<-128x1024 f32 x2 | 3.8, 1900 | 0.5 <-DVE Dm L1057 0.5
L1191 POOL TENSOR_TENSOR Y<-Y,nr_y 128x1024 f32<-128x1024 f32 x2 | 3.8, 1898 | 9.8 <-DVE nr_y L237 9.8
```

One takes 1.90 us on POOL, and on DVE 1.22 to 1.47 in the kernel before. Worse, POOL idles 9.8 us in its queue before the second ones, waiting for DVE with its masks queued behind them: merge to merge is 66.5 us in e16. In e17 `mp` of B1 still waits for the merge, 2.7 us, and merge to merge is 52.4 for 52.6. Both rivals were right. None of the eighteen kernels is measurably faster than the one before.

## Why the prediction was wrong

**B1, the step that failed.** "The waits removed sum to 2.24 + 0.78 + 0.60 + 0.47 and 1.7 for the clock" gave -6; measured, with the stretch ahead of it, is **+4.4**, an error of 10.4 of the 23 us between -9 and +14. The rows were read rightly: LX came right behind B0's merge (at 243.84 instead of 250.42), the group norm left the chain, and the waits of 2.24, 0.60 and 0.47 went. What the step did not ask is what is late next. `su` of the scan is: 2.05 us behind `hn` and `Dt`, and e8 and e13 give it back. Then the wait at issue of 0.78, which I counted as removed with its neighbours, is not a wait of this work at all: it belongs to the number of the instruction (e5, e11), moved from Tp to Q2p and grew to 1.90. So from B0's `mp` to B1's `mp` PE's waits sum to 5.8 us, where they were 4.5. And the clock, counted as 1.7 won, was lost: 10.2 us at half clock in that stretch, where the kernel before had 3.4 us, behind `mp`. This is not one profile's chance: the stretch ahead of B1 loses 3.3 to 3.5 in the six kernels with 17 slots and 5.1 to 9.7 in the eleven named at e8, and B1 itself 6.9 to 8.2 with the order of before (before, e2, e4, e10) and 8.3 to 10.2 with the new one (after, e1, e3, e6, e9, e12, e14, e15, e18).

**B2.** "I take +4"; measured +5.7. DVE's work between the merges was sized rightly, 51.5 us, and 49.96 are busy. But B2 was to hold its place "only if DVE is idle for 1.1 us in all", and DVE idles 61.60 - 49.96 = 11.6 us there, 6.1 of them right behind B1's merge, where before the group norm lay; I had looked for idle time in the old order alone. B2's merge comes 61.6 us behind B1's, against 52.6; of the 9.0 us more, DVE's work is 7.5 (42.46 us before) and its idle time 1.5. The sign that the prediction had named for a higher time, that PE loses more in B2 than B1 gained, came true, since B1 gained nothing. The rival of the bare chain named the waits at the copies and the clock rightly (13.8 us at half clock, four stretches), but not its cause: cover put back gained nothing (e12, e14, e18), DVE's load taken out, or the group norm put back, gained 2.0 against e3 (e15, e8). Its time, 1329, was met because B1's gain was missing and the second net lost 4, not because B2 cost 17.

**B3.** -4, measured -3.2, and -4.1 in e2. The twelve sums stand between Qp and Np without a wait, and 10.2 us run at half clock for 14, that is, one stretch went. The end of -8, with the clock full up to `mp`, did not come: the row from 375 has 0.66, and PE's longest wait there was 1.80 us.

**The end of the projection.** -3, measured +1.6. The two first waits became one of 2.52 at `ptr`, followed by 6.9 us at half clock where there were 3.3. e2 shows that B3's gain is paid back between its `mp` and the gate products even with 17 slots. That the sums drawn forward are what is missing there stays likely and is not shown (e10, e11).

**At nothing.** B0 was not looked at, and lost 1.6 in this profile, with two stretches at half clock for one; but e4 lost 1.3 more than before there with the old order, and e1 and e9 no more than before with the new one, so that a loss in B0 is not shown. The second feed-forward net lost 4.2: "swaps of neighbours alone" was taken as harmless, and one of them put a sum that waits 2.77 us for a load ahead of a split that PE waits for. e3 shows the cause by removing it. The descriptor space at nothing was right (e4).

**What stays open.** Why the ten runs of e3 spread by 17 us, and by how much the waits for instructions and the half clock each make up the rest of the chains' loss: the 64 passes put in moved the waits (e5, e11), and no variant was free of them. From B0's first Qp to B3's first `mp` the half clock came to 17 to 30 us in the six kernels with 17 slots and to 30 to 54 in the thirteen with 20 (e7 left out); what of this is cause and what follows from the waits, no run separates.
